# A hybrid decoder trunk on one core: attention masks ahead of the scores, and two HGRN2 levels scored in one group

## The chip, the core and the metric

The kernel runs on one core of one Trainium2 chip. The metric is the time of one execution on the device in microseconds (us), less being better. Each time is a median of several runs, with the lowest and the highest beside it.

Five engines work side by side, each through a queue of its own in a fixed order: TensorE (PE in the profile, with its weight loads as PEld), VectorE (DVE), ScalarE (ACT), GpSimd (POOL) and SyncE (SP, which here issues DMAs). They wait for each other only where data or a buffer asks for it.

## What is computed

Two layers work on 512 tokens of 1024 channels. Each is a SwiGLU feed-forward block with half weight, a mixer, and a second such block. The mixer projects the normalised stream once, splits the columns over three token mixers, and projects their joined outputs back:

```python
h = rms_norm(x, mix_norm[l]) @ w_mix_in[l]
(c_x, c_b, c_c, h_q, h_f, h_i, h_g, f_q, f_k, f_v, f_f) = jnp.split(h, split_at, axis=-1)
y = jnp.concatenate([
    short_conv_mixer(c_x, c_b, c_c, conv_w[l]),
    hgrn2_mixer(h_q, h_f, h_i, h_g, lower_bounds[l], hgrn_out_gain[l]),
    fox_mixer(f_q, f_k, f_v, f_f, fox_f_bias[l], fox_q_gain[l], fox_k_gain[l]),
], axis=-1)
x = x + y @ w_mix_out[l]
```

Two of them matter here. HGRN2 (4 heads of 64) is a gated linear recurrence in chunks of 64 tokens; within a chunk each pair of tokens is weighted by its own decay per channel, and between chunks a state is carried:

```python
scores = einsum('bhtd,bhsd,bhtsd->bhts', qb, kb, decay)      # decay = exp(bcum_t - bcum_s), causal
o = einsum('bhts,bhsv->bhtv', scores, vb) + einsum('bhtd,bhdv->bhtv', qb * exp(bcum), state)
```

The forgetting attention ("FoX", 8 heads of 64) is a causal softmax attention with normalised q and k and a decay on the logits:

```python
s = einsum('bhqd,bhkd->bhqk', qb, kh) + (cb[..., :, None] - cum[..., None, :])
s = where(qpos[:, None] >= kpos[None, :], s, MASK_VALUE)
p = softmax(s, axis=-1)
```

## The kernel before

**Dense products.** Every product with a weight matrix is done in three products of float32 halves (`mm3`, lines 450, 456 and 457): rounded high part by high part, high by low, and low by high. Weights arrive by DMA in a tile `st`, ScalarE rounds the high part into `hl` (the "hl cast", line 434) and VectorE subtracts to get the low part (the "hl subtraction", line 437). There are three `hl` buffers. In the stretches that matter, each product has 512 columns of tokens. Eight PSUM banks are named by use (line 21): three `mm`, two `sc`, two `pt`, one `po`, each kind taken in turn.

**The mixer of a layer** (`mix`, from line 1135) first projects the HGRN2 inputs, then runs two `hgrn` generators (one for each pair of heads, called a and b below) in turn with a third generator, `fox_qkv`, that holds the dense projections of the attention's q, k and v in half-granules. The loop stands at lines 1238 to 1250. After each step of an `hgrn` generator a counter goes up; where it lies in `HGRN_BESIDE`, 3 to 22 (line 24), one dense half-granule follows, which is 12 products of 512 columns. After step 8 `fox_decay` is issued (the cumulated log decays, written as `negc` by lines 1596 and 1597 and sent out by one DMA on SP).

**An hgrn generator**, after the gates: a transpose and small products give each chunk's contribution to the state; ScalarE copies them out of PSUM (line 1429) and spreads the chunk decays (line 1432); a scan on VectorE (line 1433) makes the states `S`. Then come the scores within a chunk. Pairs of tokens are split by levels 0 to 6: level 0 is a token with itself, level 1 is two neighbours, level n two halves of blocks of 2^n tokens. A level's operands are made by `operands(lev)`:

- level 0: one product q·k on VectorE (line 1451)
- level 1: an exponential of `lf` on ScalarE, then two half-tile products (1455 with q, 1456 with k)
- levels 2 to 6: an addition and a subtraction (1462, 1463), one exponential, and the product `e2` (1467)

Levels 0 and 1 are then scored by eight small TensorE products against a fixed matrix `heads2` (line 1482, eight columns of an `sc` bank in all), and written to the score tile A by a product with a mask (level 0, line 1489) or a predicated copy (level 1). Levels 2 to 6 take sixteen products of 64 rows and 32 columns (line 1513) into two `sc` banks, and two predicated copies (line 1521), one for each head. Each level is one step of the generator. The operands of the next level are asked for after a level's small products and before its copies to A. With level 1 a tile `lk` is taken anew: it lies on the storage of `lf` and `k`. ScalarE copies the states into it (line 1499) and four DMAs on SP move halves of it and of the decayed q between partitions (1501 to 1504). Temporaries come from a ring of eight tiles, the tag "t".

**The attention** (`fox_attend`) works on (head, p) with p = 0 and 1: p=0 covers the first two blocks of 128 queries, p=1 the last two. `scores(h, p)` makes for each block u a product QA·KA and a product QB·KB into the same bank, then adds the causal mask by a bf16 product of an identity `identb` with `maskb` (−1e30 above the diagonal) on the diagonal block: one product of 128 columns for each u in p=1, and one of 256 columns for both blocks in p=0, whose scores share a bank. All of these are at line 1717. A maximum, an exponential and the scaling follow (1731 to 1739), then `turn` transposes the weights (1754) and splits them in high and low (1759, 1760), and `values` multiplies by V (1772). After the last head `fo`, `fyh` and `fyl` (1785 to 1790) feed the output projection. `E` keeps these matmuls in the written order on PE; `BESIDE` (line 26) says how many dense steps stand between two attention steps.

**What sets the order.** Within each engine instructions stand in an order that is fixed when the program is built. It follows the order of the source and the priorities given there: the hl casts and subtractions are asked for with a high priority and so move ahead of small work of the mixers.

Of the kernel before, what the change touches and what calls it, by code (L numbers as in the profile page):

```python
# [8 lines left out]
F32 = mybir.dt.float32  # L9
# [190 lines left out]
def halves(x):  # L200

    return x.rearrange("p (h t) -> p h t", h=2)
# [7 lines left out]
class Trunk:  # L210
# [920 lines left out]
    def mix(self, l, w, w_out, conv_w, out_gain, q_gain, k_gain, f_bias, next_gain, logits):  # L1131
# [3 lines left out]
        with tc.tile_pool(name=self.n("mix"), bufs=1) as mp:  # L1135
# [46 lines left out]
                return bs  # L1182

            with tc.tile_pool(name=self.n("hg"), bufs=1) as hp:
                self.tt, self.tb = "t", 8

                b, kb, q, S = (pair(mp, tag) for tag in ("b", "kb", "q", "S"))
                negc = mp.tile([NH, 2, T], F32R, tag="n", name=self.n("negc"))
                bz = features([(H_F, 256)], ("mm", "mm"), lambda: self.end_norm(self.bank("pt"), hp))
                if l == 0:  # L1190
                    self.lower_bounds(logits, hp.tile([P, T], F32, tag="t", name=self.n("lb"), bufs=8))
# [163 lines left out]
    def hgrn(self, l, pr, hp, z, q, v, sg, og, S, kb, b):  # L1355
# [90 lines left out]
        def operands(lev):  # L1446
            w, half = 2**lev // 2, halves(lev)
            e = tmp()
            if lev == 0:

                nc.vector.tensor_mul(e, q, k)
                return e, None
            if lev == 1:
                self.act(half(e, 1), half(lf, 1), AF.Exp)
                nc.vector.tensor_mul(half(e, 1), half(e, 1), half(q, 1))
                nc.vector.tensor_mul(half(e, 0), half(e, 1), half(k, 0))
                return e, None
# [8 lines left out]
            e2 = tmp()[:, : T // 2]  # L1466
# [7 lines left out]
        yield  # L1474
        for lev in range(7):
            w, half = 2**lev // 2, halves(lev)
            e, e2 = ready
            sb = self.bank("sc")
            if lev < 2:
                for c in range(NCH):  # L1480
                    r = slice(CH * (c % 2), CH * (c % 2) + CH)
                    nc.tensor.matmul(
                        sb[r, c // 2 : 8 : 4], e[:, c * CH : (c + 1) * CH], self.heads2,
                        start=True, stop=True,
                    )
                d = sb[:, :8].unsqueeze(2)
                ready = operands(lev + 1)
                if lev == 0:
                    nc.vector.tensor_mul(
                        A8, self.same.unsqueeze(1).to_broadcast([P, 8, CH]), d.to_broadcast([P, 8, CH])  # L1490
# [1 line left out]
                else:  # L1492
                    m = self.lmask[:, 0, 1::2].unsqueeze(1).to_broadcast([P, 8, CH // 2])
                    nc.vector.copy_predicated(A8[:, :, 1::2], m, d.to_broadcast([P, 8, CH // 2]))


                    lk = own("lk", [P, 2 * NCH - 1, HD])
                    S2, sx, qx = lk[:, : NCH - 1], lk[:, NCH - 1 : 3 * NCH // 2 - 1], lk[:, 3 * NCH // 2 - 1 :]
                    nc.scalar.copy(S2, S[:, :, : NCH - 1].rearrange("p v c -> p c v"))
                    q4 = qe.rearrange("p (i two t) -> p i two t", two=2, t=CH)  # L1500
                    nc.sync.dma_start(qx[:64, 1:], q4[64:, 1:, 0, :])
                    nc.sync.dma_start(qx[64:], q4[:64, :, 1, :])
                    nc.sync.dma_start(sx[:64, 1:], S2[64:, 1::2])
                    nc.sync.dma_start(sx[64:], S2[:64, ::2])
                yield
                continue

            sb = [sb, self.bank("sc")]
            for i in range(4):
                for hh, par in ((0, 0), (1, 1), (0, 1), (1, 0)):  # L1510
                    r = slice(64 * hh, 64 * hh + 64)
                    c = 2 * i + par
                    nc.tensor.matmul(
                        sb[hh][CH * par : CH * par + CH, 32 * i : 32 * i + 32],
                        e[r, c * CH : (c + 1) * CH], e2[r, 32 * c : 32 * c + 32],
                        start=True, stop=True,
                    )
            if lev < 6:
                ready = operands(lev + 1)
            for hh in range(2):  # L1520
                nc.vector.copy_predicated(
                    half(A[:, hh].rearrange("p i t -> p (i t)"), 1).rearrange(
                        "p (g n) w -> p g n w", g=4
                    ),
                    half(self.lmask[:, lev - 1, :], 1).unsqueeze(1).to_broadcast([P, 4, 32 // w, w]),
                    sb[hh][:, : T // 4].rearrange("p (g n w) -> p g n w", g=4, w=w),
                )
            yield


# [162 lines left out]
    def fox_attend(self, pool, half, g):  # L1693
# [10 lines left out]
        def scores(h, p):  # L1704
# [6 lines left out]
                at = [b[:, :P], b[:, P : 3 * P]]  # L1711
            else:
                at = [self.bank("sc")[:, : 3 * P], self.bank("sc")]
            for u in range(2):
                i = 2 * p + u
                c, n = slice(i * P, (i + 1) * P), (i + 1) * P
                mm = lambda *a, **k: E(nc.tensor.matmul(*a, skip_group_check=True, **k))  # L1717
                mm(at[u], QA[:, c], KA[:, :n], start=p == 1 or u == 0, stop=False)
                mm(at[u], QB[:, c], KB[:, :n], start=False, stop=False)
                if p == 1:  # L1720
                    mm(at[u][:, c], self.identb, self.maskb, start=False, stop=True)
                elif u == 1:

                    mm(
                        b.rearrange("p (b t) -> p b t", t=P)[:, ::2, :], self.identb,
                        self.maskb.unsqueeze(1).to_broadcast([P, 2, P]), start=False, stop=True,
                    )
# [213 lines left out]
```

## Time and profile before

| | |
|---|---|
| median of 3 runs | 1765.61 us (1765.13 to 1765.96) |
| profiled execution | 1765.18 us |
| its span, first to last instruction | 1763.4 us |
| granted TensorE clock | 1.00 |
| HGRN2 beside the q, k, v projections, layer 1 | about 385 to 455 us of the span |
| attention beside V, convolution and output, layer 1 | about 455 to 517 us |
| the same in layer 2 | some 870 us later |

How to read its rows. A row of the timeline gives the start in us of the span, the time of the group in us, engine, line, operation, the tile written and those read (out<-in), the shapes, and xN, the number of instructions drawn together; a bracket at the end is the idle time before it and what ended it. For matmuls the time overlaps with the next one: the distance of two starts is what a product costs in a full stream. A row of the windows gives from:to, then for PE, PEld, DVE, ACT and POOL the busy us with the number of instructions, then the granted clock, the DMA share and GB/s.

### The profile page before, as it was taken

The page shows a single profiled execution, that of the slowest core. Times are in us where ns is not written, and L with a number is a line of the kernel's source. Part 1 is how long each engine was busy: PE and PEld are TensorE (multiplying, and loading weights), DVE is VectorE, ACT ScalarE, POOL GpSimd, SP SyncE. Part 2 cuts the span into 40 slices and gives each one's busy share as a digit, 9 for nine tenths or more (in the row PEclk, how much of TensorE's full clock was granted, in tenths as well). Part 3 has the DMA queues.
Part 4 walks back from the last instruction along what each step waited for, and adds up shares of the span by engine and source line. Part 5 has one row for each costly group of instructions (what it writes and reads, how often), then busy time and mean ns, then how long its engine had stood idle before and what let it go on. Part 6 is the DMA issues. An engine that isn't in the chain of part 4 may idle for free.

```text
span 1763.4 us, 33424 instructions
## 1 busy us (share of the span) xinstructions
PE 1755.4 (100%) x13613; PEld 1642.7 (93%) x13613; DVE 1414.5 (80%) x1956; ACT 1017.3 (58%) x1433; POOL 177.0 (10%) x174
## 2 busy tenths in 40 slices
PE   9999999999999999999999999999999999999999
PEld 7999999888888899999989999998878889999998
DVE  7988788678777898888688888876878779888793
ACT  5565565465666565565446556555657655655652
POOL 0011120100000111112001111201000001120200
PEclk9999999999999999999999999999999999999999
DMA  7768784243543776878267787923435438687762
GB/s 204 192 139 195 186 177 105 73 121 89 133 115 105 212 169 157 200 170 172 84 188 168 177 185 184 184 70 82 128 88 131 120 106 217 156 176 195 162 138 96
DMA packets 257466, 262.34 MB, mean 149 GB/s; under 512 B 25833, under 2 KB 236529, under 8 KB 257313
## 3 DMA queue, kind: packets, MB, share of 16 engines
q1 hardware_dynamic: 201456, 192.02, 37.0%
q0 software_dynamic: 55840, 68.19, 24.1%
q8 instruction: 107, 1.75, 0.4%
q14 instruction: 47, 0.38, 0.1%
q10 hardware_dynamic: 16, 0.00, 0.0%
HBM read 226.15 MB, written 2.17 MB: 129 GB/s over the span
## 4 chain that ended last, share of the span: by engine, by line
PE 94%; DVE 3%; ACT 2%; DMA 1%; issue 1%; SPq 0%; ACTq 0%; DVEq 0%
PE mm L450 13%; PE mm L456 13%; PE mm L457 13%; PE sc L457 6%; PE sc L450 6%; PE sc L456 6%; PE pt L450 6%; PE pt L457 6%; PE pt L456 6%; PE po L450 4%; PE po L456 4%; PE po L457 4%; PE sc L1717 1%; PE po L1772 1%; PE pt L1754 1%; DVE hl L437 1%
## 5 line engine op out<-in xcount | busy, mean ns | idle before, releaser
L915 DVE TENSOR_TENSOR hl<-w,hl 128x1024 fp32r<-128x1024 f32 x279 | 340.5, 1221 | 90.8 <-ACT hl L913 88.8
L913 ACT CAST hl<-w 128x1024 fp32r<-128x1024 f32 x279 | 292.7, 1049 | 198.0 <-PE mm L457 56.6
L437 DVE TENSOR_TENSOR hl<-st,hl 128x1024 fp32r<-128x1024 f32 (+3 forms) x152 | 160.0, 1053 | 102.1 <-ACT hl L434 100.6
L434 ACT CAST hl<-st 128x1024 fp32r<-128x1024 f32 (+3 forms) x151 | 137.6, 911 | 165.6 <-PE po L457 64.6
L450 PE MATMUL mm<-xc,hl 128*128 128x256 f32 x698 | 191.8, 275 | 0.4 <-ACT u L1033 0.4
L457 PE MATMUL mm<-xc,hl 128*128 128x256 f32 x696 | 191.8, 276 | 0.0
L456 PE MATMUL mm<-xc,hl 128*128 128x256 f32 x696 | 191.7, 275 | 0.0
L456 PE MATMUL pt<-xc,hl 128*128 128x256 f32 x544 | 149.9, 276 | 0.0
L450 PE MATMUL pt<-xc,hl 128*128 128x256 f32 x546 | 149.9, 275 | 0.0
L457 PE MATMUL pt<-xc,hl 128*128 128x256 f32 x544 | 149.8, 275 | 0.0
L450 PEld LDWEIGHTS mm<-xc,hl 128*128 128x128 f32 x698 | 134.1, 192 | 0.7 <-ACT u L1033 0.6
L457 PEld LDWEIGHTS mm<-xc,hl 128*128 128x128 f32 x696 | 133.8, 192 | 0.4 <-DVE hl L915 0.4
L456 PEld LDWEIGHTS mm<-xc,hl 128*128 128x128 f32 x696 | 133.8, 192 | 0.0
L450 PE MATMUL sc<-xc,hl 128*128 128x256 f32 (+1 forms) x466 | 127.9, 275 | 0.1
L457 PE MATMUL sc<-xc,hl 128*128 128x256 f32 x464 | 128.0, 276 | 0.0
L456 PE MATMUL sc<-xc,hl 128*128 128x256 f32 x464 | 127.9, 276 | 0.0
L450 PE MATMUL mm<-x,hl 128*128 128x512 f32 x272 | 106.0, 390 | 0.0
L450 PEld LDWEIGHTS pt<-xc,hl 128*128 128x128 f32 x546 | 104.8, 192 | 0.0
L457 PEld LDWEIGHTS pt<-xc,hl 128*128 128x128 f32 x544 | 104.6, 192 | 0.0
L456 PEld LDWEIGHTS pt<-xc,hl 128*128 128x128 f32 x544 | 104.5, 192 | 0.0
L457 PE MATMUL mm<-x,hl 128*128 128x512 f32 x272 | 103.2, 379 | 0.0
L456 PE MATMUL mm<-x,hl 128*128 128x512 f32 x272 | 103.2, 379 | 0.0
(520 smaller groups left out, 5596.7 us busy)
## 6 DMA issues: line engine op xcount, KB each, us to landing
w<-in_ffn_w_in_dram SPq DMA_DIRECT2D x124, 512.0 KB, 6.1
w<-in_ffn_w_out_dram POOLq DMA_DIRECT2D x50, 512.0 KB, 9.7
w<-in_ffn_w_out_dram SPq DMA_DIRECT2D x49, 512.0 KB, 5.7
st<-in_ffn_w_out_dram SPq DMA_DIRECT2D x39, 512.0 KB, 3.8
st<-in_w_mix_in_dram SPq DMA_DIRECT2D x72, 256.0 KB, 3.1
st<-in_ffn_w_in_dram SPq DMA_DIRECT2D x70, 256.0 KB, 4.0
w<-in_ffn_w_in_dram POOLq DMA_DIRECT2D x29, 512.0 KB, 9.3
w<-S POOLq DMA_DIRECT2D x29, 512.0 KB, 5.1
```

The source lines that it names most:

```text
L434: a = nc.scalar.copy(hi, src[:, c : c + w])
L437: b = nc.vector.tensor_sub(lo, src[:, c : c + w], hi)
L450: i = nc.tensor.matmul(acc[:, c], ah, bh[:, c.start // 2 : c.stop // 2, :], start=first and c.start == 0, stop=False, skip_group_check=True,)
L456: nc.tensor.matmul(acc, ah, bl, start=False, stop=False, skip_group_check=True)
L457: i = nc.tensor.matmul(acc, al, bh, start=False, stop=last, skip_group_check=True)
L913: A(nc.scalar.copy(hi, src))
L915: return lambda: V(nc.vector.tensor_sub(lo, src, hi))
L1717: mm = lambda *a, **k: E(nc.tensor.matmul(*a, skip_group_check=True, **k))
L1754: E(nc.tensor.transpose(tb[:, k * P : (k + 1) * P], to[u][:, j * P : (j + 1) * P], self.ident))
L1772: E(nc.tensor.matmul(self.ob[:, o], half[2][:, j, h].rearrange("p a d -> p (a d)"), part[:, at[0] : at[-1] + 1, :].rearrange("p b t -> p ( ...
```

## The change

Two things are changed.

**The masks.** In `scores` the mask products now come first and open the bank (`start=True`); the two products of each block are added to them. For p=1 the two masks of 128 columns stand directly behind each other, for p=0 the one of 256 columns stands ahead of both blocks. Before, each block's first product opened its bank and the mask came last.

**The levels.** `LEVELS` groups the levels; levels 0 and 1 form one group, the others have one each. A group's small products are issued together (levels 0 and 1 into eight columns each of one bank), then its writes to A. The operands of levels 0 and 1 are both made before the first step of scoring, those of level 2 are asked for ahead of level 0's write to A. The state copy and its DMAs follow the first group. An `hgrn` generator has one step less, so `HGRN_BESIDE` becomes a tuple of counts: none after the first two steps, one after the next six, two after two steps, one after ten (20 half-granules as before). The ring of temporaries has ten tiles. The sharing of `e2` in one tile by two levels (`asked`) applies to groups of several levels above 1, of which there are none.

```diff
-HGRN_BESIDE = range(3, 23)
+LEVELS = ((0, 1), (2,), (3,), (4,), (5,), (6,))
+HGRN_BESIDE = (0, 0) + (1,) * 6 + (2,) * 2 + (1,) * 10
...
-                self.tt, self.tb = "t", 8
+                self.tt, self.tb = "t", 10
...
-                        if step in HGRN_BESIDE:
+                        for _ in range(HGRN_BESIDE[step - 1] if step <= len(HGRN_BESIDE) else 0):
                             next(dense)
...
-        ready = operands(0)
+        ready = [operands(lev) for lev in LEVELS[0]]
         yield
-        for lev in range(7):
...
+        for g, levels in enumerate(LEVELS):
+            now, ready = ready, []
+            asked.clear()
+            later = list(LEVELS[g + 1]) if g + 1 < len(LEVELS) else []
+            sb = [self.bank("sc") for _ in range(2 if g else 1)]
+            for at, lev in enumerate(levels):
+                score(lev, now[at], sb, at)
+            for at, lev in enumerate(levels):
+                if later:
+                    ready.append(operands(later.pop(0)))
+                place(lev, sb, at)
+            ready += [operands(lev) for lev in later]
+            if g == 0:
+
+                lk = own("lk", [P, 2 * NCH - 1, HD])
+                S2, sx, qx = lk[:, : NCH - 1], lk[:, NCH - 1 : 3 * NCH // 2 - 1], lk[:, 3 * NCH // 2 - 1 :]
+                nc.scalar.copy(S2, S[:, :, : NCH - 1].rearrange("p v c -> p c v"))
...
             yield
...
+            mm = lambda *a, **k: E(nc.tensor.matmul(*a, skip_group_check=True, **k))
+            if p == 0:
+                masked = [b.rearrange("p (b t) -> p b t", t=P)[:, ::2, :]]
+            else:
+                masked = [at[u][:, (2 + u) * P : (3 + u) * P] for u in range(2)]
+            for m in masked:
+                mask = self.maskb.unsqueeze(1).to_broadcast([P, 2, P]) if p == 0 else self.maskb
+                mm(m, self.identb, mask, start=True, stop=False)
             for u in range(2):
                 i = 2 * p + u
                 c, n = slice(i * P, (i + 1) * P), (i + 1) * P
-                mm = lambda *a, **k: E(nc.tensor.matmul(*a, skip_group_check=True, **k))
-                mm(at[u], QA[:, c], KA[:, :n], start=p == 1 or u == 0, stop=False)
-                mm(at[u], QB[:, c], KB[:, :n], start=False, stop=False)
-                if p == 1:
-                    mm(at[u][:, c], self.identb, self.maskb, start=False, stop=True)
-                elif u == 1:
-
-                    mm(
-                        b.rearrange("p (b t) -> p b t", t=P)[:, ::2, :], self.identb,
-                        self.maskb.unsqueeze(1).to_broadcast([P, 2, P]), start=False, stop=True,
-                    )
+                mm(at[u], QA[:, c], KA[:, :n], start=False, stop=False)
+                mm(at[u], QB[:, c], KB[:, :n], start=False, stop=True)
```

`score` and `place` hold the small products and the writes to A that stood in the loop before, with a column offset for each level of the group.

More of the change, by code (lines that the diff above doesn't have):

```diff
@@ L1190, in mix @@
                 if l == 0:
-                    self.lower_bounds(logits, hp.tile([P, T], F32, tag="t", name=self.n("lb"), bufs=8))
+                    self.lower_bounds(logits, hp.tile([P, T], F32, tag="t", name=self.n("lb"), bufs=10))
                 bg = features([(H_G, 256)], ("mm", "po"))
@@ L1451, in operands @@
                 nc.vector.tensor_mul(e, q, k)
-                return e, None
+                return e
             if lev == 1:
@@ L1456, in operands @@
                 nc.vector.tensor_mul(half(e, 0), half(e, 1), half(k, 0))
-                return e, None
+                return e
             n2 = T // (2 * w)
@@ L1464, in operands @@
             self.act(e, e, AF.Exp)
-            e2 = tmp()[:, : T // 2]
+            if len(asked) % 2 == 0:
+                asked.append(tmp())
+            else:
+                asked.append(asked[-1])
+            e2 = asked[-1][:, (len(asked) - 1) % 2 * (T // 2) :][:, : T // 2]
             nc.vector.tensor_mul(
@@ L1470, in operands, with score @@
             return e, e2
-        ready = operands(0)
-        yield
-        for lev in range(7):
-            w, half = 2**lev // 2, halves(lev)
-            e, e2 = ready
-            sb = self.bank("sc")
+        asked = []
+        def score(lev, e, sb, at):
+            if lev > 1:
+                e, e2 = e
             if lev < 2:
@@ L1482, in hgrn, with place @@
                     nc.tensor.matmul(
-                        sb[r, c // 2 : 8 : 4], e[:, c * CH : (c + 1) * CH], self.heads2,
+                        sb[0][r, 8 * at + c // 2 : 8 * at + 8 : 4], e[:, c * CH : (c + 1) * CH],
+                        self.heads2, start=True, stop=True,
+                    )
+                return
+            for i in range(4):
+                for hh, par in ((0, 0), (1, 1), (0, 1), (1, 0)):
+                    r, c = slice(64 * hh, 64 * hh + 64), 2 * i + par
+                    nc.tensor.matmul(
+                        sb[hh][CH * par : CH * par + CH, P * at + 32 * i : P * at + 32 * i + 32],
+                        e[r, c * CH : (c + 1) * CH], e2[r, 32 * c : 32 * c + 32],
                         start=True, stop=True,
                     )
-                d = sb[:, :8].unsqueeze(2)
-                ready = operands(lev + 1)
+        def place(lev, sb, at):
+            w, half = 2**lev // 2, halves(lev)
+            if lev < 2:
+                d = sb[0][:, 8 * at : 8 * at + 8].unsqueeze(2)
                 if lev == 0:
@@ L1494, in hgrn @@
                     nc.vector.copy_predicated(A8[:, :, 1::2], m, d.to_broadcast([P, 8, CH // 2]))
[L1497 to L1516, printed above, removed]
-                    )
-            if lev < 6:
-                ready = operands(lev + 1)
+                return
             for hh in range(2):
@@ L1525, in hgrn @@
                     half(self.lmask[:, lev - 1, :], 1).unsqueeze(1).to_broadcast([P, 4, 32 // w, w]),
-                    sb[hh][:, : T // 4].rearrange("p (g n w) -> p g n w", g=4, w=w),
+                    sb[hh][:, P * at : P * at + P].rearrange("p (g n w) -> p g n w", g=4, w=w),
                 )
+        ready = [operands(lev) for lev in LEVELS[0]]
+        yield
+        for g, levels in enumerate(LEVELS):
[14 more added lines that the diff above has]
+                nc.scalar.copy(S2, S[:, :, : NCH - 1].rearrange("p v c -> p c v"))
+                q4 = qe.rearrange("p (i two t) -> p i two t", two=2, t=CH)
+                nc.sync.dma_start(qx[:64, 1:], q4[64:, 1:, 0, :])
+                nc.sync.dma_start(qx[64:], q4[:64, :, 1, :])
+                nc.sync.dma_start(sx[:64, 1:], S2[64:, 1::2])
+                nc.sync.dma_start(sx[64:], S2[:64, ::2])
             yield
```

2 lines of the change are left out of this document (1 added, 1 removed).

## The prediction

> **What bounds the kernel now.** I read the busy times on the page first, then PE's waits.
>
> ```profile
> PE 1755.4 (100%) x13613; PEld 1642.7 (93%) x13613; DVE 1414.5 (80%) x1956; ACT 1017.3 (58%) x1433; POOL 177.0 (10%) x174
> ```
>
> TensorE is busy for 1755.4 us, 100% of the span as the page rounds it, so an edit counts only in two ways: by the time that it adds to or takes from PE's queue of instructions, or by a wait that it gives PE. The second is rare now. This is one of the largest of PE's waits (total us, times, the longest):
>
> ```profile
> PE mm L456 <- DVE fyl L1790: 0.9, 2, 0.4
> ```
>
> It falls once in each layer, at the end of the attention, where the output product waits for the last head. It matters below.
>
> The profiled execution took 1765.18 us, 0.4 below the median of 1765.61 (runs 1765.13 to 1765.96); the sums start from 1765.18. About 0.2%, 3.5 us, can be told from no change.
>
> **Part A: the masks of the attention.** No product is added or removed. What changes is what stands before and behind each mask product. These are the scores of a p=1 step in the timeline (start, us), products on PE first and then two weight loads on PEld:
>
> ```profile
> 471.95 0.42 PE L1717 MATMUL sc<-S,S 128*128 128x384 f32 x1
> 472.21 0.34 PE L1717 MATMUL sc<-q,q 66*128 66x384 f32 x1
> 472.39 0.23 PE L1717 MATMUL sc<-maskb,identb 128*128 128x128 bf16 x1
> 472.43 0.48 PE L1717 MATMUL sc<-S,S 128*128 128x512 f32 x1
> 472.75 0.40 PE L1717 MATMUL sc<-q,q 66*128 66x512 f32 x1
> ```
> ```profile
> 472.39 0.10 PEld L1717 LDWEIGHTS <-identb 128*128 128x128 bf16 x1 [0.16 <-issue]
> ...
> 472.52 0.19 PEld L1717 LDWEIGHTS sc<-q,q 66*128 66x128 f32 x1
> ```
>
> A dense stream of 512-column products starts one every 0.216 us (398.02, 398.24 in the rows of part B); 128 columns are a quarter of that, 0.054, and 384 are 0.162. From the q product at 472.21 to the one at 472.75 are 0.54 us. Taking off 0.162 for the first and 0.216 for the S product, **0.16 us** is the mask. There are two such masks in a p=1 step. The product itself is 0.054 of that; the other 0.106 are loads, which I halve: the mask's own load, which waits (0.16 us of idle put down to "issue") until the product before it is over, and the part of the next, float32 load that so short a product doesn't hide. A longer product hides a float32 load: that at 472.52 starts while the S product of 472.43 runs.
>
> Afterwards, for p=1, both masks stand at the front, behind the transposes (L1754), which have 128 columns like a mask and so leave 0.053 of the first S load exposed today: 2 × 0.16 + 0.053 = 0.373 in all. After the change the inner S load and the first load of the values (L1772) lie behind products of 384 and 512 columns, which hide them; what is left are two masks of 0.054, their loads and the first S load's 0.053. The order of the changed program still has both identity loads. If the second waits for the first mask's end, as the one at 472.39 does for the product ahead of it, that is 0.267 and saves 0.106; if it hides, 0.160. There are 14 such pairs (8 heads, 2 layers, less the first head of each, which stands behind dense 512-column products, has no exposed S load today and saves 0.053). For p=0 the one mask of 256 columns moves to the front:
>
> ```profile
> 476.84 0.28 PE L1717 MATMUL sc<-kb,kb 66*128 66x256 f32 x1
> ...
> 477.01 0.37 PE L1772 MATMUL po<-PH,V 128*128 128x256 f32 x1
> 477.21 0.28 PE L1772 MATMUL po<-PL,V 128*128 128x256 f32 x1
> ```
>
> From 476.84 to 477.21 are 0.37; less two products of 256 columns it is 0.154: 0.108 of product and 0.05 of its own load, as its 256 columns hide the next. That bears the halving out. At the front the S load's exposed rest hides behind it, so 14 × 0.054 go. **Sum of A:** 14 × 0.106 + 2 × 0.053 + 14 × 0.054 = 2.35 us, with a hidden second load 3.2; the other end is nothing saved, if each change between the number types empties PE whatever stands where. I take 2.35, as no row shows such a load hidden.
>
> The Trainium skill, "TensorE: Matmul & The Clock Gate", section "The mechanism", says that a weight load overlaps running products only where their row groups differ. The float32 row at 472.52 contradicts it, the identity row at 472.39 fits it. Held everywhere, it speaks against the change: no load would be covered by the longer products, and a pair would save some 0.05, A as a whole about 1.6.
>
> Not all of A arrives. At the layer's end the chain runs over ScalarE and VectorE to the wait on fyl quoted above (0.4 us in each layer), and what PE gains in its last 18 us (two pairs and their p=0 steps, some 0.25) is waited for there: **+0.5** for both layers.
>
> **Part B: HGRN2's levels 0 and 1 in one group.** PE's order was H0a D H0b D H1a D H1b D L2a (a, b are the two head pairs, H the small products of a level, D a dense half-granule); it becomes H0a H1a D D H0b H1b D D L2a. One switch:
>
> ```profile
> 398.02 0.38 PE L456 MATMUL mm<-hl,x 128*128 128x512 f32 x1
> 398.24 0.38 PE L457 MATMUL mm<-hl,x 128*128 128x512 f32 x1
> 398.55 0.63 PE L1482 MATMUL sc<-heads,t 128*64 128x2 f32 x16
> 399.11 0.48 PE L450 MATMUL mm<-hl,x 128*128 128x512 f32 x1
> 399.43 0.38 PE L456 MATMUL mm<-hl,x 128*128 128x512 f32 x1
> ```
>
> From 398.24 to 399.43 are 1.19; less two dense products 0.76, of which 0.56 are the small products and 0.1 each the entry and the exit. Two switches of four go in each layer: **−0.4 per layer**.
>
> The price lies on VectorE. Operands are now asked for sooner, and the changed order shows ScalarE copying the states (lk<-S, L1499) of pair a directly behind its exponential, ahead of pair b's copies. That copy writes a tile that lies on lf and k, so it must wait for VectorE's last reader of k (L1456); pair b's copies, its scan and all behind them queue up.
>
> ```profile
> 391.36 0.86 ACT L1429 COPY t<-pt 128x256 f32<-128x256 f32 x2 [1.82 <-PE pt L1423]
> 392.07 0.61 ACT L1432 COPY t<-dc 128x512 f32<-128x512 f32 x1
> 392.58 0.94 ACT L340 ACTIVATE t<-lk 128x256 f32<-128x256 f32 x2
> 394.14 1.05 ACT L434 CAST hl<-st 128x1024 fp32r<-128x1024 f32 x1 [0.62 <-PE po L457]
> 395.09 1.03 ACT L1499 COPY lk<-S 128x448 f32<-128x448 f32 x1
> 396.02 0.63 ACT L340 ACTIVATE t<-t 128x512 f32<-128x512 f32 x1
> ```
> ```profile
> 390.71 1.27 DVE L1451 TENSOR_TENSOR t<-q,lk 128x512 f32<-128x512 f32 x2
> 392.71 1.22 DVE L1433 TENSOR_TENSOR_SCAN S<-t,t 128x512 f32<-128x512 f32 x1 [0.73 <-ACT t L1432]
> 393.85 0.76 DVE L1455 TENSOR_TENSOR t<-t,q 128x256 f32<-128x256 f32 x2
> 394.53 0.75 DVE L1456 TENSOR_TENSOR t<-t,lk 128x256 f32<-128x256 f32 x2
> ...
> 397.01 0.68 DVE L1489 TENSOR_TENSOR A<-same,sc 128x512 f32<-128x512 f32 x1
> ...
> 409.86 1.22 DVE L437 TENSOR_TENSOR hl<-st,hl 128x1024 fp32r<-128x1024 f32 x1
> 411.00 0.72 DVE L1521 COPY_PREDICATED A<-lmask,sc 128x128 f32<-128x128 uint8 x2
> ```
>
> Pair a's first product ends at 391.35 (half of 1.27), L1455 and L1456 0.76 later at 392.1; then the state copy (1.03), pair b's copies (0.86) and decay (0.61): the scan starts at about 394.5 instead of 392.71. In the changed order the hl cast, which stood ahead of level 2's exponential, stands behind it: scan 1.2, L1455 0.4, L1463 (a half tile as well) 0.4 and the exponential 0.6 bring it to 397.0 instead of 394.14. Its own 1.0, the hl subtraction's 1.2 and negc's, about as long as A's product, bring A to some 400.1 instead of 397.01, 3.1 late. Some 1.8 us of that is work brought ahead of A (by half tiles of 0.4: L1467 of pair a, L1462 and L1463 of pair b; and negc): VectorE is **1.3 behind**. It has no room to catch up:
>
> ```profile
> 397.01:411.72 14.71, 14.71 (x136) 12.04 (x134) 14.12 (x39) 10.52 (x24) 0.00 (x0) 1.00 0.45 103
> ```
>
> VectorE is busy for 14.12 of 14.71 us there (third pair of figures; the granted clock is 1.00). At its end stands level 2 of pair a: its two copies (411.00 to 411.72) free the banks for level 2 of pair b, so PE waits for both, and the changed order puts the hl subtraction between them, which moves only the first.
>
> ```profile
> 411.99 0.67 PE L1513 MATMUL sc<-t,t 64*64 64x32 f32 x32
> ...
> 432.30 0.67 PE L1513 MATMUL sc<-t,t 64*64 64x32 f32 x32
> ```
>
> Before, PE came 0.27 after the copies. Now it comes at 411.58 without a wait (0.4 of switches saved) and the second copy ends near 411.72 + 1.25 = 412.95: a stall of 1.37, **+0.96 per layer** net of the 0.4. It has its bounds at no stall (VectorE makes the lag up, with the 0.59 us that it is idle there and more) and 3.2 (the full 3.1 arrives: 414.8 − 411.58). I take 1.37, nearest to the queue's own rows. Level 5 repeats the pattern:
>
> ```profile
> 430.31 0.48 DVE L1521 COPY_PREDICATED A<-lmask,sc 128x128 f32<-128x128 uint8 x2
> 430.74 1.23 DVE L437 TENSOR_TENSOR hl<-st,hl 128x1024 fp32r<-128x1024 f32 x1
> ```
>
> There the copies stood ahead of hl and now stand around it: the second ends at 432.2 and, with the lag, 433.6, against PE at 432.30 + 0.96 = 433.3: **+0.3 per layer**. Level 2 of pair a, both pairs of level 3 and the dense products' own hl keep over 0.8 us of cover by the same reckoning. The temporaries' ring of ten buffers, the fewer steps (dense halves are 20 as before) and SP's order (negc's DMA stands behind the states' four) cost nothing as long as VectorE, not a buffer, is late: each is needed a stage later. The second layer repeats the first.
>
> **Sum:** −2.35 + 0.5 + 2 × (0.96 + 0.3) = +0.67, from 1765.18: **1765.8 us**, about no change.
>
> **Rivals.** *VectorE keeps up.* For it: 0.59 us of idle time, and a stall of 1.37 is a small difference of times reckoned through some 40 instructions. Against: the 14.12 of 14.71. B gives −0.8 then, and the sum is 1765.18 − 2.35 + 0.5 − 0.8 = 1762.5; with the second identity load hidden 1761.7. *The whole lateness arrives*, the slower side. The place is again the second copy of level 2 of pair a; the price is the 3.1 instead of 1.3, if the work brought forward ran in time that VectorE had free before 397.01 anyhow while it waited for ScalarE; then 1.8 more in each layer, 1765.8 + 3.6 = 1769.4. It decides from a lag of about 3 on. For it: ScalarE's 0.73 us of wait ahead of the scan shows VectorE idle there already. Against: only 0.7 of such idle time stands in the rows, not 1.8. *Masks side by side save nothing*: each change of type empties PE. Only B stays: 1765.18 + 2.52 = 1767.7, within 0.2%. This is also the case that the change doesn't do what it says, as the second load of the same identity stays in the order.
>
> **How the numbers follow.** The forecast (a stall of about one lag at level 2, A about 2.35) has 0.57; the masks without effect 0.12, within 0.2% too but for 0.01 where 0.8 us of lag comes on top in each layer; VectorE keeping up 0.21, which lies below 1765.61 − 3.5 = 1762.1 only where the second load hides too or the tail's 0.5 is kept (0.12 of it; 0.09 stays within 0.2%); the whole lateness 0.10. Faster 0.12, same 0.77, slower 0.11. The range runs from 1762.0, which leaves out about 0.1, to 1768.3 (the masks without effect, with 0.3 us more of lag in each layer), which leaves out the other 0.1.
>
> **What would show it.** In the changed trace: q product to q product in p=1 at 0.38 instead of 0.54; the mask pair standing directly behind the transposes with a second identity load exposed or not; a VectorE wait of about 1.4 us in each layer ahead of level 2 of pair b (near 412 and 870 us later); the scan of pair b near 394.5. PE reaching that product without a wait would make B wrong, an unchanged distance of the q products A.

## The result and the profile after

| | before | after |
|---|---|---|
| median | 1765.63 us (1764.66 to 1767.10, 22 runs) | 1767.68 us (1766.23 to 1770.03, 22 runs) |
| profiled execution, span | 1765.18, 1763.4 us | 1767.66, 1765.8 us |

The change makes the kernel slower by a factor of 1.0013, with a 95% interval of 1.0007 to 1.0019: 2.05 us, clear of the noise of so many runs, and inside the 0.2% that the prediction called no change.

In the lines of the changed kernel, 438 is the hl subtraction, 1494 the small products of levels 2 to 6, 1514 their predicated copies, 1540 the state copy and 1732 the scores with their masks. The busy times of the page come first:

```profile
PE 1753.9 (99%) x13613; PEld 1645.1 (93%) x13613; DVE 1416.6 (80%) x1956; ACT 1016.5 (58%) x1433; POOL 177.0 (10%) x174
```

PE works 1.5 us less than before, and the span is 2.4 us longer. So the time went into waits, and PE's waits (total us, times, the longest) show which ones are new:

```profile
PE sc L1494 <- DVE ft L597: 2.2, 2, 1.1
...
PE sc L1494 <- DVE A L1514: 0.6, 2, 0.3
```

Two waits of 1.1 and two of 0.3 us stand ahead of a small product, one of each in each layer; the wait for fyl in the attention is 0.9 us in all, as it was. Two longer waits of the first 11 us (line 504 after, 503 before) leave nothing behind: at 100 us the same dense product starts 0.07 us earlier than in the kernel before. The releaser "ft" of the longer one is the instruction that VectorE ended last, not the reason: that is the predicated copy just ahead of it, as the next two views show. PE in layer 1, from level 2 of pair a to level 3 of pair a:

```profile
408.01 0.67 PE L1494 MATMUL sc<-t,t 64*64 64x32 f32 x32
...
411.74 0.30 PE L1494 MATMUL sc<-t,t 64*64 64x32 f32 x2 [0.27 <-DVE A L1514]
413.13 0.66 PE L1494 MATMUL sc<-t,t 64*64 64x32 f32 x30 [1.09 <-DVE ft L597]
...
415.00 0.63 PE L458 MATMUL mm<-hl,x 128*128 128x512 f32 x1
415.43 0.63 PE L451 MATMUL mm<-hl,x 128*128 128x512 f32 x1
...
418.13 0.68 PE L1494 MATMUL sc<-t,t 64*64 64x32 f32 x32
```

VectorE over the same stretch and before it:

```profile
394.69 1.23 DVE L1434 TENSOR_TENSOR_SCAN S<-t,t 128x512 f32<-128x512 f32 x1 [1.24 <-ACT t L1433]
...
400.30 0.67 DVE L1506 TENSOR_TENSOR A<-same,sc 128x512 f32<-128x512 f32 x1
...
411.26 0.43 DVE L1514 COPY_PREDICATED A<-lmask,sc 128x128 f32<-128x128 uint8 x1
411.48 1.26 DVE L438 TENSOR_TENSOR hl<-st,hl 128x1024 fp32r<-128x1024 f32 x1
412.65 0.43 DVE L1514 COPY_PREDICATED A<-lmask,sc 128x128 f32<-128x128 uint8 x1
```

Pair b's first products start at 411.74 behind the first copy, and the other 30 at 413.13 behind the second, which ends at 413.08; the hl subtraction stands between. Behind this wait the reader sees something that the prediction doesn't have: seven dense products (415.00 to 417.56) start 0.43 us apart instead of 0.216. The window table says why (us, then busy us of PE, PEld, DVE, ACT, POOL, then the granted clock):

```profile
412.00:433.00 21.00, 19.91 (x254) 15.88 (x254) 17.66 (x54) 11.66 (x23) 1.04 (x2) 0.92 0.26 77
1283.00:1305.00 22.00, 20.61 (x266) 16.59 (x265) 20.03 (x59) 13.60 (x29) 1.03 (x2) 1.00 0.24 74
```

In layer 1 PE's clock fell to half for some 3.4 us (0.92 as a mean of 21 us); in layer 2, after the same wait, it did not. Layer 2 therefore shows the wait's own price. These are the small products of pair a, level 2 and then level 3, in the kernel before and in the changed one:

```profile
1278.94 0.67 PE L1513 MATMUL sc<-t,t 64*64 64x32 f32 x32
...
1285.71 0.49 PE L1513 MATMUL sc<-t,t 64*64 64x32 f32 x20
```
```profile
1280.67 0.67 PE L1494 MATMUL sc<-t,t 64*64 64x32 f32 x32
...
1289.19 0.67 PE L1494 MATMUL sc<-t,t 64*64 64x32 f32 x32
```

The changed kernel is 1.73 us late at the first and 3.48 at the last: **the wait costs 1.75 us**. In layer 1 it is 0.59 early at level 2 (408.60 became 408.01) and 2.76 late at level 3 (415.37 became 418.13): 3.35, of which 1.6 is the slow clock. The same dense product compared in both traces goes from +2.77 at the start of layer 1's attention to +2.17 near its end (543 us of the kernel before), and in layer 2 from +3.48 to +2.88: the masks won about 0.6 us in each layer.

Finally a p=1 step of the attention, on PE (compare 471.95 to 473.24):

```profile
508.19 0.93 PE L1771 MATMUL pt<-ident,P 128*128 128x128 f32 x7
508.96 0.28 PE L1732 MATMUL sc<-maskb,identb 128*128 128x128 bf16 x2
509.04 0.43 PE L1732 MATMUL sc<-A 128*128 128x384 f32 x1
509.31 0.34 PE L1732 MATMUL sc<-kb,kb 66*128 66x384 f32 x1
509.49 0.40 PE L1732 MATMUL sc<-A 128*128 128x512 f32 x1
509.73 0.40 PE L1732 MATMUL sc<-kb,kb 66*128 66x512 f32 x1
509.97 0.28 PE L1789 MATMUL po<-PH,V 128*128 128x256 f32 x1
510.09 0.28 PE L1789 MATMUL po<-PL,V 128*128 128x256 f32 x1
```

The scores' products now follow each other without a gap, 0.24 us for 512 columns. The transposes start 0.77 us ahead of the first mask, though, where before the first score product followed them after 0.68.

### The profile page after: what moved, and what is told of

Read it like the earlier page. It is cut to its first block, busy times and chain, and to the rows that moved or that the text cites. A ratio compares the mean times of both kernels' runs of the same rounds, so it can differ in the third digit from the quotient of the medians.

```text
span 1765.8 us, 33420 instructions
## 1 busy us (share of the span) xinstructions
PE 1753.9 (99%) x13613; PEld 1645.1 (93%) x13613; DVE 1416.6 (80%) x1956; ACT 1016.5 (58%) x1433; POOL 177.0 (10%) x174
## 3 DMA queue, kind: packets, MB, share of 16 engines
q8 instruction: 107, 1.75, 0.4%
HBM read 226.15 MB, written 2.17 MB: 129 GB/s over the span
## 4 chain that ended last, share of the span: by engine, by line
PE 87%; DVE 7%; ACT 2%; DMA 2%; issue 1%; SPq 0%; ACTq 0%; DVEq 0%
PE mm L451 13%; PE mm L457 12%; PE mm L458 12%; PE sc L458 6%; PE sc L457 6%; PE sc L451 6%; PE pt L457 6%; PE pt L451 6%; PE pt L458 6%; PE po L457 3%; PE po L458 3%; PE po L451 3%; DVE hl L438 2%; PE sc L1732 1%; PE po L1789 1%
```

## The experiments

The theory after the result: the loss is PE's wait for the second copy of level 2 of pair a, which comes from ScalarE's order (the state copy ahead of pair b's copies makes VectorE late) together with VectorE's (the hl subtraction between the copies); falls of the clock that follow such a wait add 1.6 us each; the masks win 1.2 us. The main rival: grouping is harmless and the loss lies elsewhere. The medians, with the intervals of the ratio to the kernel before on the same chip:

| run | median us | before | ratio, interval | runs with granted clock 1.000 / 0.999 / 0.998 / 0.997 |
|---|---|---|---|---|
| changed kernel | 1767.68 | 1765.63 | 1.0013 [1.0007, 1.0019] | 11 / 10 / 1 / 0 |
| masks only | 1764.63 | 1765.68 | 0.9994 [0.9985, 1.0003] | 11 / 0 / 0 / 0 |
| levels only | 1770.27 | 1765.68 | 1.0023 [1.0013, 1.0033] | 3 / 3 / 3 / 0 |
| copies first | 1765.43 | 1765.68 | 0.9996 [0.9987, 1.0005] | 11 / 0 / 0 / 0 |
| state copy later | 1764.01 | 1765.68 | 0.9988 [0.9979, 0.9997] | 11 / 0 / 0 / 0 |
| both mends | 1763.28 | 1766.03 | 0.9986 [0.9977, 0.9995] | 11 / 0 / 0 / 0 |
| masks left out | 1762.48 | 1766.03 | 0.9980 [0.9971, 0.9989] | 10 / 0 / 0 / 0 |
| three repeats | 1771.17 | 1766.03 | 1.0027 [1.0016, 1.0039] | 1 / 1 / 4 / 0 |
| four repeats | 1770.31 | 1766.03 | 1.0025 [1.0016, 1.0034] | 6 / 1 / 4 / 0 |
| four, dense products tied | 1771.69 | 1765.54 | 1.0036 [1.0025, 1.0048] | 0 / 2 / 4 / 1 |
| nine, dense products tied | 1770.70 | 1765.54 | 1.0027 [1.0017, 1.0037] | 7 / 1 / 0 / 0 |

### The masks alone

The attention of the changed kernel, all else as before.

> Only the masks are moved; HGRN2 stays as before. My reading of the changed trace: a p=1 step is 0.06 us shorter, a p=0 step the same, so the two layers together win some 1.0 to 1.2 us: 1764.5 against 1765.6. The sum of the prediction for this part (2.35 less 0.5) gives 1763.8. The rival that a mask costs the same wherever it stands gives 1765.6.

1764.63, 1.05 us less; the interval doesn't exclude zero by itself, but the size is that of the traces, and not the prediction's 1.85: from the transposes to the next dense product the 14 p=1 steps that hold scores are 1.09 us shorter in all in this trace, and 1.05 in the changed kernel's.

### The levels alone

```diff
-            for m in masked:
-                mm(m, self.identb, mask, start=True, stop=False)
...
+                if p == 1:
+                    mm(at[u][:, c], self.identb, self.maskb, start=False, stop=True)
```

> Only the levels are grouped; the masks stay last. Theory of the wait: switches -0.6 and a wait ahead of level 2 of pair b of 1.4 us or a little more in each layer, net +1.15 per layer, +2.3 together, and 1.6 more for each layer in which PE's clock falls to half after the wait: 1767.9, 1769.5 or 1771.1, the median near 1769. The prediction's sum for this part gives 1768.1 with no falls of the clock. Rival: the loss lies elsewhere (in the attention's new order), then this is at 1764.4, the 1.2 of switches saved.

1770.27: 4.6 us more than before, so the rival is out. The wait is there in both layers (0.30 + 1.09 and 0.28 + 1.09), and the nine runs had nine falls in their 18 layers: three runs with two, three with one, three with none. 2.3 + 1.6 is 3.9; the remaining 0.7 is inside the interval.

### Both copies ahead of the subtraction

```diff
             for hh in range(2):
+              with self.tc.high_priority():
                 nc.vector.copy_predicated(
```

> The changed kernel, but the predicated copies of levels 2 to 6 get a high priority, so that on VectorE both of level 2 of pair a stand ahead of the hl subtraction again; ScalarE's order, with the state copy ahead of pair b's, stays. If the place of the subtraction between the two copies makes the wait: they end near 411.7, the wait is at most 0.3 us, the clock does not fall, and the time is about 1763.7 (1765.6 - 1.2 for switches - 1.2 for masks + 0.5). If VectorE's lag by itself made it (whatever stands between the copies), the wait stays near 1 us and the time above 1766.

On VectorE and PE:

```profile
411.64 0.72 DVE L1515 COPY_PREDICATED A<-lmask,sc 128x128 f32<-128x128 uint8 x2
412.14 1.26 DVE L438 TENSOR_TENSOR hl<-st,hl 128x1024 fp32r<-128x1024 f32 x1
```
```profile
408.32 0.67 PE L1494 MATMUL sc<-t,t 64*64 64x32 f32 x32
...
412.13 0.94 PE L1494 MATMUL sc<-t,t 64*64 64x32 f32 x32 [0.35 <-DVE A L1515]
...
415.79 0.87 PE L1494 MATMUL sc<-t,t 64*64 64x32 f32 x32
```

VectorE is as late as in the changed kernel (pair b's scan at 395.00 in a run that is 0.3 later throughout), and yet the wait is down to 0.35 us and no run shows a fall. The loss is not down to 0.35, though: from level 2 of pair a to that of pair b are 3.81 us and on to level 3 of pair a 3.66, instead of 3.39 each, and this last group itself takes 0.87 instead of 0.67. Layer 1 loses 0.9 in all, layer 2 0.84. The time is 2.25 us below the changed kernel's, though 1.7 above the 1763.7 that was expected; that sum allowed 0.5 for the waits, and the trace shows 1.74, which accounts for 1.2 of the 1.7. The rest is open; that the priority itself costs it is unlikely, as the run with both mends below has it too.

### The state copy later

```diff
+        self.spread = nc.scalar.copy(dec3, dc.unsqueeze(1).to_broadcast([P, HD, NCH]))
...
+                s2 = nc.scalar.copy(S2, S[:, :, : NCH - 1].rearrange("p v c -> p c v"))
+                self.tc.add_manual_dep(s2.ins, self.spread.ins.name, NOSYNC, reason="given order")
```

> The changed kernel, but the state copy of pair a is made to follow pair b's copies and decay on ScalarE; VectorE's order, with the subtraction between the two copies, stays. If the queue behind the state copy made VectorE late: pair b's scan starts near 393.2 instead of 394.7, the second copy ends some 1.4 us sooner, near 411.7, the wait is gone, 1763.2. If the place of the subtraction alone makes the wait, the scan moves and the wait stays at 1.2 us or more, with the time above 1766.

```profile
410.60 0.43 DVE L1514 COPY_PREDICATED A<-lmask,sc 128x128 f32<-128x128 uint8 x1
410.83 1.26 DVE L438 TENSOR_TENSOR hl<-st,hl 128x1024 fp32r<-128x1024 f32 x1
412.00 0.42 DVE L1514 COPY_PREDICATED A<-lmask,sc 128x128 f32<-128x128 uint8 x1
```
```profile
408.77 0.67 PE L1494 MATMUL sc<-t,t 64*64 64x32 f32 x32
412.15 0.99 PE L1494 MATMUL sc<-t,t 64*64 64x32 f32 x32
```

The subtraction is still between the copies, but all of it comes earlier. This run is 0.76 us later than the changed one at level 2 of pair a (408.77 against 408.01), and its second copy 0.65 earlier (412.00 against 412.65): 1.4 us against PE, as expected. Level 2 of pair b starts 3.38 us after that of pair a, the regular distance, and its group takes 0.99 instead of 0.67: some 0.3 of wait is left inside it. So the long wait needs both causes, but they don't weigh the same: a layer loses 1.75 us with both, 0.9 where VectorE is late and the copies stand together, 0.33 where the subtraction stands between them and VectorE is in time. 1764.01 against the expected 1763.2.

### Both mends

> The changed kernel with both mends: the state copy of pair a behind pair b's copies on ScalarE, and both predicated copies of a level ahead of the hl subtraction on VectorE. If the two causes share one wait, which each mend alone has taken away but for 0.3 us, there is little left to win: 0.3 us per layer at most over the mended ScalarE order (1764.0), so 1763.4 to 1764.0, and a granted clock of 1.000 in all runs. If the high priority of the copies costs something elsewhere (the run with it alone came to 1765.4, 1.4 above the other mend), this lies near 1765.

**1763.28 us**, ratio 0.9986: faster than both kernels. Level 2 of pair b runs without a wait:

```profile
410.46 0.72 DVE L1515 COPY_PREDICATED A<-lmask,sc 128x128 f32<-128x128 uint8 x2
```
```profile
412.00 0.67 PE L1494 MATMUL sc<-t,t 64*64 64x32 f32 x32
415.38 0.67 PE L1494 MATMUL sc<-t,t 64*64 64x32 f32 x32
```

1.2 of switches and 1.05 to 1.2 of masks make 2.3 to 2.4; the median of before less that of this kernel is 2.75.

### The masks left out

```diff
-                if p == 1:
-                    mm(at[u][:, c], self.identb, self.maskb, start=False, stop=True)
-                elif u == 1:
...
```

> The kernel before with all 48 mask products left out, so that the attention is not causal; each block's first product still opens its bank. Prices the masks where they stood. By the distances in the traces, with 0.24 us for 512 columns in these products, a mask costs 0.11 to 0.13 us: 48 x 0.12 = 5.8 us less, some 0.3 of it lost to the wait at the layer's end: 1760.2. By the price in the prediction (0.16 and 0.154) 7.6 less, 1758.4.

1762.48, only 3.55 less, so neither number holds. In the trace a p=1 step without a wait is 0.23 to 0.26 us shorter than before, some 0.12 for each mask, as the distances gave:

```profile
506.13 0.93 PE L1746 MATMUL pt<-ident,P 128*128 128x128 f32 x7
506.81 0.42 PE L1717 MATMUL sc<-A 128*128 128x384 f32 x1
...
508.13 0.43 PE L450 MATMUL mm<-hy,hl 128*128 128x512 f32 x1
```

2.00 us from the transposes to the dense product; before it was 2.24 (505.75 to 507.99 at the same place). Of 48 × 0.12 = 5.8 us some 2.2 are given back: the wait for fyl grows from 0.44 to 0.71 and from 0.43 to 0.70, and ahead of the scores at 1356 us PE has two new waits of 0.3 us, for an exponential and for a DMA of the operands; where the rest went is open. Even without masks the attention's PE time can't all be won.

### What makes the clock fall

The copies first, or the changed kernel, with repeats of the second copy of level 2 of pair a:

```diff
+                for _ in range(3 if lev == 2 and pr == 0 and hh == 1 else 0):
+                  with self.tc.high_priority():
+                    nc.vector.copy_predicated(
...
```

> The changed kernel with the copies at high priority, and three repeats of the second copy of level 2 of pair a behind it, which change nothing in A but hold the bank. PE's wait ahead of level 2 of pair b becomes 1 to 2.5 us. If PE's clock falls after such a wait by the length of the wait: falls about as often as in the changed kernel or more often (half or more of the runs below a clock of 1.000). If the falls came from something else in the changed kernel (its ScalarE order, its masks, which are all in the version with the copies first, where all runs had 1.000), there are none here. Time: 1765.4 + 2 x wait + 1.6 per fall, 1768 to 1772.

> The changed kernel with four repeats of the second copy of level 2 of pair a, spread over the next instructions of VectorE: PE's wait grows from 1.4 to 3 us or more. If the clock falls by the length of the wait against a window of some 3.4 us: a fall in nearly every layer, all runs at 0.998, and the time near 1767.1 + 2 x 2 + 3.2 = 1774. If a fall is a matter of chance whatever the wait: half of the layers, as in the changed kernel, near 1772.5.

Neither got what was meant: in the built order three and six dense products now stand between the two halves of level 2 of pair b, so the waits were 0.3 and then 1.36, and 0.3 and then 1.47 us, hardly longer than the changed kernel's. Two more kernels tied the first dense product behind the small ones to them:

```diff
+            if getattr(self, "hold", None):
+                self.tc.add_manual_dep(i.ins, self.hold, NOSYNC, reason="given order")
...
```

> The changed kernel with the copies at high priority, four repeats of the second copy of level 2 of pair a, and the dense products behind level 2 of pair b tied to their place, so that PE's wait is in one piece: the repeats end some 1.2 (hl subtraction) + 5 x 0.2 + 0.4 after the copies, so the wait is about 2.5 to 3 us in each layer, twice that of the changed kernel. If a longer idle time makes the fall of the clock likelier: 15 or more of about 20 layers fall, runs mostly at 0.998, time 1765.4 + 2 x 2.5 + 3 = 1773. If a fall is as likely with any such wait: about half of the layers, 1772.

> As the kernel with four repeats, but with nine: the wait grows by some 5 x 0.2 + 0.6 to about 4.5 us in each layer. If the clock is decided by the idle share of a stretch of 3 to 4 us, each layer falls, all runs at 0.998, and the slow stretch stays at some 3 us: 1765.4 + 2 x 4.2 + 3.2 = 1777. If a fall is as likely with any such wait, half of the layers and 1775.

The tie didn't keep the halves together either. PE with four repeats:

```profile
412.28 0.66 PE L1497 MATMUL sc<-t,t 64*64 64x32 f32 x16 [0.27 <-DVE A L1520]
...
415.71 0.66 PE L1497 MATMUL sc<-t,t 64*64 64x32 f32 x16 [1.49 <-DVE ft L600]
```

Nine repeats gave three short waits, of 0.29, 0.27 and 0.82 us in layer 1. A mean clock of 0.999 is one fall (half speed for some 3.4 us is 0.001 of the span), 0.998 two, and each fall is put down to one of the two layers, which only the profiled runs show. Counted so over layers and runs:

| longest wait in a layer, us | layers that fell |
|---|---|
| 0.35 or less (copies first) | 0 of 22 |
| 0.82 (nine repeats) | 1 of 16 |
| 1.09 (changed; levels only) | 12 of 44; 9 of 18 |
| 1.36 (three repeats) | 9 of 12 |
| 1.47 (four repeats) | 9 of 22 |
| 1.49 (four, tied) | 12 of 14 |

One run with the tie has 0.997, three falls in two layers; the third, whose place is not known, is left out. So falls come with waits of about a microsecond and more and not with short ones, and the shares above that don't follow the length alone.

The profiled runs show what goes with a fall between two equal waits. The slow stretches in them are all 3.413 us long, and the stretches at full speed between them are whole multiples of that (120 and 395 times in the changed kernel, 119, 255 and 140 with three repeats). So in these traces the clock changes only on a grid of 3.413 us, which lies differently in each run. In the changed kernel (columns as in the window table above):

```profile
411.39:414.80 3.41, 2.05 (x38) 1.71 (x38) 3.41 (x12) 1.39 (x5) 0.00 (x0) 1.00 0.26 59
414.80:418.21 3.41, 3.41 (x13) 2.22 (x15) 3.25 (x12) 0.63 (x1) 0.00 (x0) 0.50 0.25 95
...
1281.79:1285.20 3.41, 2.63 (x13) 1.89 (x11) 3.41 (x7) 1.76 (x5) 0.00 (x0) 1.00 0.24 91
1285.20:1288.61 3.41, 2.80 (x40) 2.52 (x41) 3.41 (x17) 1.35 (x4) 0.00 (x0) 1.00 0.50 154
```

In layer 1 the whole wait, 1.36 us, lies in one stretch of the grid, and the next stretch is slow. In layer 2 the border at 1285.20 cuts the same wait into 0.8 and 0.6, and nothing falls. The other traces fit: with the levels only, 0.30 and 1.09 fell into two stretches in layer 1 (no fall), and 1.37 into one in layer 2 (fall); 1.36 to 1.50 in one stretch was followed by a fall in both layers with three repeats and with four tied. The one exception by idle time is layer 1 of four repeats, 1.47 us without a fall. By what PE took in, it is none: counting a product at 0.216 us for 512 columns, the six stretches ahead of a fall hold 1.16 to 1.41 us of work, that one 1.46, and every other one in the twelve traces, the start and the end of the program left aside, more than 1.5. The margin is thin, no run set the position of the grid, and a single wait of 3 us was not made; but the traces support the idle share of such a stretch, as the expectation for nine repeats put it, and not the length of the wait alone.

## Why the prediction came out as it did

**The bound was right.** PE was full, and only its own queue and one new wait moved the time.

**The wait ahead of level 2 of pair b was right in its place and its price.** ScalarE's rows of the changed kernel:

```profile
392.47 1.05 ACT L1540 COPY lk<-S 128x448 f32<-128x448 f32 x1 [2.51 <-DVE t L1457]
393.42 0.73 ACT L1430 COPY t<-pt 128x256 f32<-128x256 f32 x2
394.05 0.61 ACT L1433 COPY t<-dc 128x512 f32<-128x512 f32 x1
```

The scan was forecast at 394.5 and came at 394.69; A at 400.1, and it came at 400.30; the end of the second copy at 412.95, and it came at 413.08; PE's wait at 1.37, and it was 0.27 + 1.09. The experiments confirm both links of that chain. The price on the path is 1.75 and not 1.37, as PE was there 0.2 earlier than reckoned and two of 32 products had already been let in.

**The switches** were put at 0.4 per layer and gave 0.55 in layer 1 (408.60 became 408.01, of which 0.04 stood there before the levels) and 0.48 in layer 2 (+2.21 at the small products of 1260.95, +1.73 at level 2). So layer 2, without a fall, lost 1.75 − 0.48 = 1.27, against a forecast of 0.96 + 0.3 = 1.26: the sum is met by luck, as the 0.3 did not come and the first wait cost 0.4 more.

**The second wait, at level 5, did not come.** The pattern did, as VectorE's rows show:

```profile
432.98 0.29 DVE L1514 COPY_PREDICATED A<-lmask,sc 128x128 f32<-128x128 uint8 x1
433.17 1.22 DVE L438 TENSOR_TENSOR hl<-st,hl 128x1024 fp32r<-128x1024 f32 x1
434.31 0.28 DVE L1514 COPY_PREDICATED A<-lmask,sc 128x128 f32<-128x128 uint8 x1
```

PE came for these banks only at 435.07. In layer 2, without a fall, the second copy ended at 1305.65 and PE came at 1306.12. The step that failed added VectorE's whole lag of 1.3 a second time: the wait at level 2 had already made PE late by as much (1.27 in layer 2, 2.8 with the fall in layer 1), and VectorE was no longer behind it.

**The masks were over-priced, and the term A is the one that was mis-sized:** 2.35 less 0.5 was forecast, 1.05 came in the run with the masks alone. The step took the rate of the dense stream, 0.216 us for 512 columns, for products that need up to 0.24 (509.49, 509.73, 509.97). So a mask at the end cost not 0.16 but 0.53 − 0.18 − 0.24 = 0.11, and from q product to q product are now 0.42 us (509.31 to 509.73) and not the 0.38 that was named as a sign. And the front was too cheap: transposes to first S product took 0.85 (508.19 to 509.04), against 0.68 without masks there (506.13 to 506.81 in the kernel that leaves them out), 0.17 for the pair. 2 × 0.11 less 0.17 leaves 0.05 in this p=1 step; over all 14 it is 0.04 to 0.10, 0.075 in the mean, against a forecast of 0.106. p=0 gains next to nothing, against a forecast of 0.054 each: from its transposes to the next group of transposes are 1.80 us before (509.99 to 511.79) and after (500.75 to 502.55), and all 14 together gain some 0.1. Of the rest, the first mask's load took its 0.09 at the front, behind the transposes; the second cost PE nothing that shows (S follows 0.08 us after the first of the two masks), so the case of the hidden second load was the true one in a sum that was too large. The Trainium skill's rule in "TensorE: Matmul & The Clock Gate", section "The mechanism", gave 0.05 per pair, nearer to the 0.075 that came than the 0.106 of the sum, but not for its reason: the rows still show float32 loads under running products, and the gaps between the scores' products are gone.

**The +0.5 for the wait on fyl did not come, and its place was misread.** The wait stands halfway through the attention, where the output product needs the second pair of heads; attention goes on beside the output projection up to the transposes at 550.51, and not only to 517. PE before and after:

```profile
516.30 0.48 PE L456 MATMUL mm<-fyl,hl 128*128 128x512 f32 x1 [0.44 <-DVE fyl L1790]
```
```profile
518.75 0.48 PE L457 MATMUL mm<-fyl,hl 128*128 128x512 f32 x1 [0.47 <-DVE fyl L1807]
```

It grew by 0.03 us in layer 1 and by 0.01 in layer 2, so the masks' gain was not waited away there. The 1.05 is thus to be held against the whole 2.35.

**The clock was not in the prediction at all.** In the changed kernel the runs at a clock of 1.000 have a mean of 1767.08 and those at 0.999 one of 1768.67: 1.6 us for a fall, as in layer 1 of the trace. Twelve falls in 22 runs are 0.9 us per run. The Trainium skill, the same page, section "HAM oscillation — how this bites in real kernels", says that PE stays at full clock if it has no idle gaps of more than about 3.4 us. The trace disagrees: 0.27 and 1.09 us with two products between were enough where both lay in one stretch of the grid.

So the sum of +0.67 was made of a wait that was right, a second wait that was not there (0.6 too much), masks that won 0.65 to 0.8 too little against 2.35 less 0.5, and falls of the clock of 0.9 that were not in it. The median of 1767.68 lies inside the range because these partly cancel, not because each term was good.

## What to carry to other kernels

Where TensorE is full, follow a change through the queues of the other engines as they are built: here an edit that takes PE work away moved one copy on ScalarE by a few places, and VectorE arrived 1.3 us late at the one place where PE had 0.27 us in hand. Price a product by its own neighbours in the trace and not by the densest stream in it, and count a lag once: after PE has waited for it, it is gone. A new wait of about a microsecond can cost more than itself through the clock, so take the small waits out (both mends: 1763.28 us) before judging the idea.

## What the runs showed of the hardware

TensorE's clock fell to half for 3.413 us after waits of 1.1 to 1.5 us, in 51 of 110 layers that had one (counted by the mean clock of a run), and in 1 of 38 with waits of 0.8 us or less; each fall cost about 1.6 us. In the profiled runs the falls stand on a grid of 3.413 us, and a fall followed where PE had 1.36 to 1.50 us of idle time within one stretch of it, but for one case of 1.47; the same wait cut in two by the grid did nothing. None of the 73 runs of the kernel before in the three series of experiments shows one. The scores' products take 0.22 to 0.24 us for 512 columns and the values' 0.12 for 256, where dense products take 0.216 and 0.11; why is open.
